# HGRN unit of a hybrid encoder block: inverse running products by scans, and a state chain with one VectorE operation per chunk

## The chip, the cores and the metric

The kernel runs on one core of a Trainium2 chip. A core has five engines that each work through a queue of their own in order: TensorE (PE, matmuls; PEld is its loading of weights), VectorE (DVE), ScalarE (ACT), GpSimd (POOL) and SyncE (SP, which here only issues transfers). They meet through semaphores. The metric is the device time of one execution in microseconds, and less is better.

## The reference

One layer of a bidirectional encoder over 1024 tokens of width 1024: a combined projection of 11776 columns, dilated attention, a gated linear recurrence (HGRN2) in both directions, a gated merge, a feed-forward part, and layer norms. The part that matters here is the recurrence. It has 8 heads with 128 keys and 128 values each, and is computed in chunks:

```python
cum = jnp.cumsum(logf.reshape(b, h, n, c, kd), axis=3)
q_dec = q * jnp.exp(cum)
k_inv = k * jnp.exp(-cum)
a = jnp.einsum('bhnik,bhnjk->bhnij', q_dec, k_inv)
a = jnp.where(causal_in_chunk, a, 0.0)
o_intra = jnp.einsum('bhnij,bhnjv->bhniv', a, v)
u = jnp.einsum('bhnck,bhncv->bhnkv', k * jnp.exp(cum_last - cum), v)
def step(state, inp):
    d, uu = inp
    return d[..., None] * state + uu, state
o_inter = jnp.einsum('bhnck,bhnkv->bhncv', q_dec, s_start)
```

So each gate f needs its running product within a chunk, the inverse of that product, and a state that is carried from chunk to chunk with one multiplication by the chunk's whole product.

## The kernel before

**Stages.** Phase 0 normalises the input (up to about 75 us of the profile). Phase 1 (up to about 1200 us) streams the combined projection: `stream` takes four column tiles at a time through a Strassen-Winograd scheme of seven block products, and every product is done as three matmuls (high x high, L244; high x low, L245; low x high, L246) over weights that are split into a rounded high part (`w_hi`, L205, ScalarE) and the rest (`w_lo`, L209, GpSimd). Four pairs of `w_hi`, `w_lo` are kept. Sums of weight blocks are made on VectorE and GpSimd (L477 to L482). Results leave the PSUM banks `pj0` to `pj3` through evacuations on VectorE (L392, L403, L417, L419) and ScalarE (L390, L500). Phases 2 and 3 are the merge and the feed-forward part.

**Side units.** Beside the projection, and on the same engines, phase 1 runs units of side work as soon as the columns that they need are there: eight HGRN units (one per head, `hgrn_side`) and eight attention units. A unit is a Python generator; each `yield n` lets `n` products of the stream be written before it goes on. The HGRN units fall, two by two, into the stretches from about 100, 400, 650 and 900 us.

**What sets the order.** The program is not written out by hand: a planner (`schedule_with_timeline_sim=True`) places each engine's instructions ahead of time by its own idea of their durations and by priority; evacuations of the projection and the preparation of weights are raised by `evac_ahead = 1000`. At run time each engine keeps the order that the planner gave it.

**An HGRN unit.** The tokens of a head lie in 8 groups of 128 along the free axis, `d` is the direction. A group is split into a near half and a far half of 64 tokens, and the running products start at the border between them, so that they stay within range. `hgrn_dir` makes the gates f on ScalarE (L930 to L936: `Identity` with scale `ga` and bias `gb` of a stored tanh) into `A` (the far half, 64 wide) and `B` (the near half, 66 wide), sets their first or last columns to zero on GpSimd (L928 to L934), and turns them into running products in place with a scan on VectorE (L942). The scan computes `state = f * state + d1`, where the table `d1` is zero but for a one at each group's start: so a zero in f and a one in `d1` restart the product. Then four reciprocals of 128x256 on VectorE (L953, L956) give the inverse products in `qd`; GpSimd multiplies the keys by `B` (L950) and by the inverse of `A` (L954), VectorE the queries by `A` (L957) and by the inverse of `B` (L958). `dec` takes the two halves' whole products of each group (L962, L963).

`hgrn_keys` transposes the keys through PSUM. `hgrn_states` makes the states that each group starts from: matmuls of keys and values into two PSUM banks (tag `sd`, of which there are four for all side work), then a chain on VectorE with two operations per group: add the decayed state before (L998) and decay the sum (L999; L996 for the first). ScalarE copies each state, scaled by `dec`, into `S` (L990). `hgrn_scores` and `hgrn_out` do the rest (L1012 to L1038). `S` of direction 0 takes the slot that held `A`, `S` of direction 1 that of `B` of direction 0.

Small buffers of 128x512 (`half`, five in rotation) are shared by the transposed keys, the scores, the output of the units and attention's bias tables.

Of the kernel before, what the change touches and what calls it, by code (L numbers as in the profile page):

```python
# [10 lines left out]
F32 = mybir.dt.float32  # L11
F32R = mybir.dt.float32r
I32 = mybir.dt.int32
AF = mybir.ActivationFunctionType
OP = mybir.AluOpType
# [19 lines left out]
CQ = 0.5 * 128 ** -0.5  # L35
# [44 lines left out]
class Block:  # L80
# [836 lines left out]

    def hgrn_dir(self, h, d, st):

        nc = self.nc  # L920
        ga, gb, gna = (z[:, d, h:h + 1] for z in (self.ga, self.gb, self.gna))
        t3 = st[f"t{d}"].rearrange("p (c i) -> p c i", i=128)
        q3 = st["q"].rearrange("p (c i) -> p c i", i=128)

        A = st["fa"][:, HALF * d:HALF * d + HALF].rearrange("p (c i) -> p c i", i=64)
        B = self.slot(7 + d, "fb", (8, 66))
        if d == 0:
            nc.gpsimd.memset(A[:, :, 0:1], 0.0)  # L928
            nc.gpsimd.memset(B[:, :, 65:66], 0.0)
            nc.scalar.activation(A[:, :, 1:64], t3[:, :, 65:128], AF.Identity, bias=gb, scale=ga)  # L930
            nc.scalar.activation(B[:, :, 0:65], t3[:, :, 0:65], AF.Identity, bias=gb, scale=ga)
        else:
            nc.gpsimd.memset(A[:, :, 63:64], 0.0)
            nc.gpsimd.memset(B[:, :, 0:1], 0.0)  # L934
            nc.scalar.activation(A[:, :, 0:63], t3[:, :, 0:63], AF.Identity, bias=gb, scale=ga)
            nc.scalar.activation(B[:, :, 1:66], t3[:, :, 63:128], AF.Identity, bias=gb, scale=ga)  # L936
        nc.gpsimd.tensor_scalar(t3, t3, gna, ga, op0=OP.mult, op1=OP.add)

        def scan(f, n, rev):
            f = f.rearrange("p c i -> p (c i)")  # L940
            f = f[:, ::-1] if rev else f
            nc.vector.tensor_tensor_scan(f, f, self.d1[n], 0.0, op0=OP.mult, op1=OP.add)  # L942

        scan(A, 64, d == 1)
        scan(B, 66, d == 0)
        far = slice(64, 128) if d == 0 else slice(0, 64)
        near = slice(0, 64) if d == 0 else slice(64, 128)
        R = B[:, :, 1:65]
        qd = self.slot(2 + 2 * d, "qd", (8, 128))
        nc.gpsimd.tensor_mul(t3[:, :, near], t3[:, :, near], R)  # L950
        yield
        for c in (slice(0, 4), slice(4, 8)):
            nc.vector.reciprocal(qd[:, c, far], A[:, c])  # L953
        nc.gpsimd.tensor_mul(t3[:, :, far], t3[:, :, far], qd[:, :, far])  # L954
        for c in (slice(0, 4), slice(4, 8)):
            nc.vector.reciprocal(qd[:, c, near], R[:, c])  # L956
        nc.vector.scalar_tensor_tensor(qd[:, :, far], q3[:, :, far], CQ, A, op0=OP.mult, op1=OP.mult)  # L957
        nc.vector.scalar_tensor_tensor(qd[:, :, near], q3[:, :, near], CQ, qd[:, :, near], op0=OP.mult, op1=OP.mult)  # L958
        st["qd", d], st["ki", d] = qd, t3

        dec = st["dec", d] = self.smt.tile([128, 2, 8], F32, name="dec", tag="dec", bufs=4)
        nc.gpsimd.tensor_copy(dec[:, 0, :], A[:, :, 63 if d == 0 else 0])  # L962
        nc.gpsimd.tensor_copy(dec[:, 1, :], B[:, :, 0 if d == 0 else 65])  # L963

    def hgrn_keys(self, st, d):

        nc, out = self.nc, []
        for b in (0, 1) if d == 0 else (1, 0):
            pt, kT = self.ps_sd(), self.half3("hkT")
            for k in range(4):  # L970
                nc.tensor.transpose(pt[:, 128 * k:128 * (k + 1)], st["ki", d][:, 4 * b + k, :], self.ident)
            nc.scalar.copy(kT, pt.rearrange("p (k c) -> p k c", k=4))
            out.append(kT)
        return out

    def hgrn_states(self, st, d, kT, vT):

        nc, dec = self.nc, st["dec", d]
        S = self.slot(6 + d, "hS", (8, 128))
        cs = list(range(8)) if d == 0 else list(range(7, -1, -1))  # L980
        E = None
        for b in range(2):
            ps = self.ps_sd().rearrange("p (k c) -> p k c", k=4)
            part = cs[4 * b:4 * b + 4]
            for jj, c in enumerate(part):
                if c != cs[-1]:
                    nc.tensor.matmul(ps[:, jj, :], kT[b][:, c % 4, :], vT[:, c, :], start=True, stop=True)  # L987
            for jj, c in enumerate(part):
                if E is not None:
                    nc.scalar.activation(S[:, c, :], E, AF.Copy, scale=dec[:, 1, c:c + 1])  # L990
                if c == cs[-1]:
                    continue

                En = self.sm.tile([128, 128], F32, name="hR", tag="hR", bufs=3)
                if E is None:
                    nc.vector.tensor_scalar(En, ps[:, jj, :], dec[:, 0, c:c + 1], None, op0=OP.mult)  # L996
                else:
                    nc.vector.scalar_tensor_tensor(En, E, dec[:, 1, c:c + 1], ps[:, jj, :], op0=OP.mult, op1=OP.add)  # L998
                    nc.vector.tensor_scalar(En, En, dec[:, 0, c:c + 1], None, op0=OP.mult)  # L999
                E = En  # L1000
        return S

    def hgrn_scores(self, st, b):
# [722 lines left out]
```

## Time and profile before

| | us |
|---|---|
| median of 3 runs (lowest, highest) | 2131.55 (2130.61, 2132.82) |
| span of the profiled execution | 2135.9 |
| TensorE busy (95% of the span) | 2032.5 |
| VectorE busy (65%) | 1386.7 |
| GpSimd busy (51%) | 1090.4 |
| ScalarE busy (43%) | 918.9 |

The profile is of one more execution; it gives its span from the first to the last instruction and no other time of it. A group's row reads: line, engine, operation, output<-inputs, shapes, count | busy us in all, mean ns of one | idle time of the engine just before them and what ended it. A row of the waits reads: engine and line that waited <- engine and line that ended the wait: us in all, times, longest. A row of a timeline reads: start, duration, engine, line, operation, and in brackets the idle time before it. Matmuls overlap, so their durations do not add up; the distance of their starts is what they cost.

### The profile page before, as it was taken

How to read it: one execution, taken by the hardware profiler on the slowest of the kernel's cores; microseconds unless marked ns; L12 is line 12 of the kernel's file. 1: busy time of each engine (PE TensorE's matmuls, PEld its weight loads, DVE VectorE, ACT ScalarE, POOL GpSimd, SP SyncE). 2: the span in 40 equal slices, each digit the busy share in tenths (PEclk: the TensorE clock that was granted, in tenths of full speed). 3: DMA queues.
4: the chain of work that ended last, by engine and by line, in shares of the span. 5: the costliest groups of instructions: out<-in, count | busy, mean ns of one | idle time of the engine just before them, and what ended most of it. 6: DMA issues, size and time to landing. Idle time of an engine off the chain costs nothing.

```text
span 2135.9 us, 30950 instructions
## 1 busy us (share of the span) xinstructions
PE 2032.5 (95%) x10941; PEld 1678.8 (79%) x10941; DVE 1386.7 (65%) x2228; ACT 918.9 (43%) x1864; POOL 1090.4 (51%) x882
## 2 busy tenths in 40 slices
PE   4799999999999999989999899999999999999998
PEld 3678787878878888868888688878788888888876
DVE  7666746776468754677536722336867677767777
ACT  6544445444554435443355332134433333334542
POOL 3465653565535764466644764353656666630012
PEclk9899999999999999999999999999999999999999
DMA  5343452434424453333433855244434334348433
GB/s 206 103 125 103 131 159 89 141 110 150 140 90 139 129 170 122 121 118 114 156 111 117 286 191 185 87 138 143 148 109 158 129 130 142 119 153 305 158 89 124
DMA packets 273885, 301.10 MB, mean 141 GB/s; under 512 B 14081, under 2 KB 205378, under 8 KB 273730
## 3 DMA queue, kind: packets, MB, share of 16 engines
q1 hardware_dynamic: 266272, 273.73, 39.9%
q10 hardware_dynamic: 7458, 25.40, 3.0%
q8 instruction: 86, 1.41, 0.3%
q14 instruction: 69, 0.57, 0.1%
HBM read 200.25 MB, written 98.83 MB: 140 GB/s over the span
## 4 chain that ended last, share of the span: by engine, by line
PE 62%; DVE 6%; issue 3%; DMA 3%; POOL 2%; ACT 1%; SPq 0%; ACTq 0%; DVEq 0%; POOLq 0%
PE pj L244 13%; PE pj L245 13%; PE pj L246 13%; PE sd L245 6%; PE sd L244 6%; PE sd L246 6%; POOL w_lo L209 1%; PE sd L1038 1%; PE sd L987 1%; DMA a<-ah 1%; DVE qd L956 1%; DVE qd L953 1%; POOL att_lo L209 0%; PE sd L643 0%; DVE hR L999 0%
## 5 line engine op out<-in xcount | busy, mean ns | idle before, releaser
L209 POOL TENSOR_TENSOR w_lo<-wa,w_hi 128x512 fp32r<-128x512 f32 x276 | 384.4, 1400 | 278.0 <-ACT w_hi L205 267.3
L205 ACT CAST w_hi<-wa 128x512 fp32r<-128x512 f32 x276 | 170.1, 618 | 231.1 <-PE pj L245 171.8
L209 POOL TENSOR_TENSOR w_lo<-wsum,w_hi 128x512 fp32r<-128x512 f32 x88 | 128.9, 1474 | 113.0 <-PE sd L246 60.7
L200 POOL TENSOR_TENSOR mv<-mv,mhalf 128x1 f32<-128x1 f32 x24 | 17.3, 723 | 228.9 <-DVE mv L199 225.7
L209 POOL TENSOR_TENSOR w_lo<-f_raw,w_hi 128x512 fp32r<-128x512 f32 x66 | 102.0, 1555 | 56.0 <-ACT w_hi L205 54.8
L244 PE MATMUL pj<-xt1hi,w_hi 128*128 128x512 f32 x260 | 105.0, 405 | 14.4 <-ACT xt1hi L205 6.9
L205 ACT CAST w_hi<-wsum 128x512 fp32r<-128x512 f32 x88 | 54.7, 621 | 124.6 <-PE sd L245 116.8
L245 PE MATMUL pj<-xt1lo,w_hi 128*128 128x512 f32 x260 | 103.5, 398 | 4.5 <-DVE xt1lo L209 4.5
L246 PE MATMUL pj<-xb22hi,w_lo 128*128 128x512 f32 x260 | 101.8, 391 | 1.6 <-POOL w_lo L209 1.6
L478 POOL TENSOR_TENSOR wa<-wa,wa 128x512 f32<-128x512 f32 x46 | 65.3, 1421 | 74.0 <-DVE ws L477 63.0
L246 PE MATMUL pj<-xt1hi,w_lo 128*128 128x512 f32 x260 | 102.9, 396 | 0.0
L244 PE MATMUL pj<-xb22hi,w_hi 128*128 128x512 f32 x260 | 102.5, 394 | 0.0
L245 PE MATMUL pj<-xb22lo,w_hi 128*128 128x512 f32 x260 | 101.8, 391 | 0.0
L209 POOL TENSOR_TENSOR w_lo<-ws,w_hi 128x512 fp32r<-128x512 f32 x46 | 67.3, 1467 | 64.2 <-ACT w_hi L205 63.9
L205 ACT CAST gwsum<-a_raw 128x512 fp32r<-128x512 f32 (+1 forms) x78 | 47.7, 616 | 100.9 <-PE pj L245 43.6
L500 ACT COPY wkeep<-pj 128x512 f32<-128x512 f32 x138 | 80.2, 581 | 11.4 <-DVE evh L392 5.9
L209 DVE TENSOR_TENSOR gwkeep<-a_raw,gwsum 128x512 fp32r<-128x512 f32 (+1 forms) x78 | 57.6, 739 | 41.1 <-ACT gwsum L205 38.2
L244 PE MATMUL pj<-xb11hi,w_hi 128*128 128x512 f32 x192 | 78.8, 412 | 4.9 <-DVE wkeep L417 3.4
L403 DVE TENSOR_TENSOR evh<-wkeep,pj 128x512 f32<-128x512 f32 x48 | 32.6, 680 | 76.4 <-PE pj L246 56.3
L244 PE MATMUL pj<-xt4hi,w_hi 128*128 128x512 f32 x192 | 77.1, 402 | 2.5 <-DVE evh L392 2.5
L246 PE MATMUL pj<-xt2hi,w_lo 128*128 128x512 f32 x192 | 75.7, 394 | 3.8 <-POOL w_lo L209 3.8
L990 ACT ACTIVATE hS<-hR,dec 128x128 f32<-128x128 f32 x112 | 44.5, 402 | 80.8 <-DVE hR L999 56.7
(406 smaller groups left out, 6608.3 us busy)
## 6 DMA issues: line engine op xcount, KB each, us to landing
wa<-in_w_in_dram SPq DMA_DIRECT2D x184, 256.0 KB, 3.1
f_raw<-in_w_ffn_in_dram SPq DMA_DIRECT2D x44, 512.0 KB, 4.2
a_raw<-gd SPq DMA_DIRECT2D x30, 512.0 KB, 3.8
gd<-fc SPq DMA_DIRECT2D x44, 256.0 KB, 2.0
gd<-fs SPq DMA_DIRECT2D x33, 256.0 KB, 2.1
tg<-evh SPq DMA_DIRECT2D x32, 256.0 KB, 2.9
tg<-tg SPq DMA_DIRECT2D x16, 512.0 KB, 3.8
y<-ahs SPq DMA_DIRECT2D x16, 512.0 KB, 5.3
```

The source lines that it names most:

```text
L205: nc.scalar.copy(hi, src)
L209: ins = e.tensor_sub(lo, src, hi.bitcast(F32))
L244: nc.tensor.matmul(ps, whi, xhi, start=first, stop=False, **kw)
L245: nc.tensor.matmul(ps, whi, xlo, start=False, stop=False, **kw)
L246: nc.tensor.matmul(ps, wlo, xhi, start=False, stop=last, **kw)
L403: nc.vector.tensor_add(t, add, ps)
L478: nc.gpsimd.tensor_sub(a["a21"], a["a11"], a["a21"])
L500: nc.scalar.copy(t, ps)
L953: nc.vector.reciprocal(qd[:, c, far], A[:, c])
L956: nc.vector.reciprocal(qd[:, c, near], R[:, c])
L987: nc.tensor.matmul(ps[:, jj, :], kT[b][:, c % 4, :], vT[:, c, :], start=True, stop=True)
L990: nc.scalar.activation(S[:, c, :], E, AF.Copy, scale=dec[:, 1, c:c + 1])
```

## The change

The diff touches `hgrn_dir` and `hgrn_states`.

In `hgrn_dir` the inverse products no longer come from reciprocals of the whole arrays. Two more buffers, `X` and `Y`, are filled with the same gates, shifted by one token, and scanned in the opposite direction, starting from the reciprocal of the group's whole product (128x8 values) in place of one. A product from the far end back to a token, divided by the whole product, is the inverse of the product up to that token. The starting values are written into the ones of the table `d1` (`first`), and a memset sets them to one again before the next direction. The queries of the near half now read `Y` instead of a part of `qd`.

In `hgrn_states` ScalarE takes each group's matmul result out of PSUM, already decayed by `dec[:, 0]`, into the slot of `S` that the next group will use. The chain on VectorE is then one operation per group, with `dec[:, 2]`, the product of the two decays, made by GpSimd. ScalarE scales the result by `dec[:, 1]` into `S`, and scales the first state in place.

```diff
+        X, Y = (self.half(n).rearrange("p (c i) -> p c i", i=64) for n in ("hx", "hy"))
+
+        def gate(out, src):
+            nc.scalar.activation(out, src, AF.Identity, bias=gb, scale=ga)
...
+            nc.gpsimd.memset(X[:, :, 63:64], 0.0)
+            nc.gpsimd.memset(Y[:, :, 0:1], 0.0)
+            gate(X[:, :, 0:63], t3[:, :, 65:128])
+            gate(Y[:, :, 1:64], t3[:, :, 1:64])
...
+        first = self.d1[64].rearrange("p (c i) -> p c i", i=64)[:, :, 0]
...
+        def inverse(f, total, rev):
+
+            nc.vector.reciprocal(first, total[:, ::-1] if rev else total)
+            scan(f, 64, rev)
+
+        nc.vector.memset(first, 1.0)
         scan(A, 64, d == 1)
         scan(B, 66, d == 0)
...
-        for c in (slice(0, 4), slice(4, 8)):
-            nc.vector.reciprocal(qd[:, c, far], A[:, c])
-        nc.gpsimd.tensor_mul(t3[:, :, far], t3[:, :, far], qd[:, :, far])
-        for c in (slice(0, 4), slice(4, 8)):
-            nc.vector.reciprocal(qd[:, c, near], R[:, c])
+        inverse(X, A[:, :, 63 if d == 0 else 0], d == 0)
+        nc.gpsimd.tensor_mul(t3[:, :, far], t3[:, :, far], X)
+        inverse(Y, R[:, :, 0 if d == 0 else 63], d == 1)
         nc.vector.scalar_tensor_tensor(qd[:, :, far], q3[:, :, far], CQ, A, op0=OP.mult, op1=OP.mult)
-        nc.vector.scalar_tensor_tensor(qd[:, :, near], q3[:, :, near], CQ, qd[:, :, near], op0=OP.mult, op1=OP.mult)
+        nc.vector.scalar_tensor_tensor(qd[:, :, near], q3[:, :, near], CQ, Y, op0=OP.mult, op1=OP.mult)
...
+        nc.gpsimd.tensor_mul(dec[:, 2, :], dec[:, 0, :], dec[:, 1, :])
...
-            for jj, c in enumerate(part):
-                if E is not None:
-                    nc.scalar.activation(S[:, c, :], E, AF.Copy, scale=dec[:, 1, c:c + 1])
-                if c == cs[-1]:
-                    continue
-
-                En = self.sm.tile([128, 128], F32, name="hR", tag="hR", bufs=3)
+            part = [(jj, c, cs[4 * b + jj + 1]) for jj, c in enumerate(cs[4 * b:4 * b + 4]) if c != cs[-1]]
+            for jj, c, _ in part:
+                nc.tensor.matmul(ps[:, jj, :], kT[b][:, c % 4, :], vT[:, c, :], start=True, stop=True)
+            for jj, c, after in part:
+                nc.scalar.activation(S[:, after, :], ps[:, jj, :], AF.Copy, scale=dec[:, 0, c:c + 1])
+            for jj, c, after in part:
                 if E is None:
-                    nc.vector.tensor_scalar(En, ps[:, jj, :], dec[:, 0, c:c + 1], None, op0=OP.mult)
+                    E = S[:, after, :]
                 else:
-                    nc.vector.scalar_tensor_tensor(En, E, dec[:, 1, c:c + 1], ps[:, jj, :], op0=OP.mult, op1=OP.add)
-                    nc.vector.tensor_scalar(En, En, dec[:, 0, c:c + 1], None, op0=OP.mult)
-                E = En
+                    En = self.sm.tile([128, 128], F32, name="hR", tag="hR", bufs=3)
+                    nc.vector.scalar_tensor_tensor(En, E, dec[:, 2, c:c + 1], S[:, after, :], op0=OP.mult, op1=OP.add)
+                    E = En
+                if after != cs[1]:
+                    nc.scalar.activation(S[:, after, :], E, AF.Copy, scale=dec[:, 1, after:after + 1])
+                    if after == cs[2]:
+                        nc.scalar.activation(S[:, cs[1], :], S[:, cs[1], :], AF.Copy, scale=dec[:, 1, cs[1]:cs[1] + 1])
```

More of the change, by code (lines that the diff above doesn't have):

```diff
@@ L926, in hgrn_dir @@
         B = self.slot(7 + d, "fb", (8, 66))
+        qd = self.slot(2 + 2 * d, "qd", (8, 128))
+        far = slice(64, 128) if d == 0 else slice(0, 64)
+        near = slice(0, 64) if d == 0 else slice(64, 128)
+        X, Y = (self.half(n).rearrange("p (c i) -> p c i", i=64) for n in ("hx", "hy"))
+        def gate(out, src):
+            nc.scalar.activation(out, src, AF.Identity, bias=gb, scale=ga)
         if d == 0:
@@ L929, in hgrn_dir @@
             nc.gpsimd.memset(B[:, :, 65:66], 0.0)
-            nc.scalar.activation(A[:, :, 1:64], t3[:, :, 65:128], AF.Identity, bias=gb, scale=ga)
-            nc.scalar.activation(B[:, :, 0:65], t3[:, :, 0:65], AF.Identity, bias=gb, scale=ga)
+            gate(A[:, :, 1:64], t3[:, :, 65:128])
+            gate(B[:, :, 0:65], t3[:, :, 0:65])
+            nc.gpsimd.memset(X[:, :, 63:64], 0.0)
+            nc.gpsimd.memset(Y[:, :, 0:1], 0.0)
+            gate(X[:, :, 0:63], t3[:, :, 65:128])
+            gate(Y[:, :, 1:64], t3[:, :, 1:64])
         else:
@@ L934, in hgrn_dir @@
             nc.gpsimd.memset(B[:, :, 0:1], 0.0)
-            nc.scalar.activation(A[:, :, 0:63], t3[:, :, 0:63], AF.Identity, bias=gb, scale=ga)
-            nc.scalar.activation(B[:, :, 1:66], t3[:, :, 63:128], AF.Identity, bias=gb, scale=ga)
+            gate(A[:, :, 0:63], t3[:, :, 0:63])
+            gate(B[:, :, 1:66], t3[:, :, 63:128])
+            nc.gpsimd.memset(X[:, :, 0:1], 0.0)
+            nc.gpsimd.memset(Y[:, :, 63:64], 0.0)
+            gate(X[:, :, 1:64], t3[:, :, 0:63])
+            gate(Y[:, :, 0:63], t3[:, :, 64:127])
         nc.gpsimd.tensor_scalar(t3, t3, gna, ga, op0=OP.mult, op1=OP.add)
+        first = self.d1[64].rearrange("p (c i) -> p c i", i=64)[:, :, 0]
         def scan(f, n, rev):
@@ L942, in scan @@
             nc.vector.tensor_tensor_scan(f, f, self.d1[n], 0.0, op0=OP.mult, op1=OP.add)
+        def inverse(f, total, rev):
+            nc.vector.reciprocal(first, total[:, ::-1] if rev else total)
+            scan(f, 64, rev)
+        nc.vector.memset(first, 1.0)
         scan(A, 64, d == 1)
         scan(B, 66, d == 0)
-        far = slice(64, 128) if d == 0 else slice(0, 64)
-        near = slice(0, 64) if d == 0 else slice(64, 128)
         R = B[:, :, 1:65]
-        qd = self.slot(2 + 2 * d, "qd", (8, 128))
         nc.gpsimd.tensor_mul(t3[:, :, near], t3[:, :, near], R)
         yield
-        for c in (slice(0, 4), slice(4, 8)):
-            nc.vector.reciprocal(qd[:, c, far], A[:, c])
-        nc.gpsimd.tensor_mul(t3[:, :, far], t3[:, :, far], qd[:, :, far])
-        for c in (slice(0, 4), slice(4, 8)):
-            nc.vector.reciprocal(qd[:, c, near], R[:, c])
+        inverse(X, A[:, :, 63 if d == 0 else 0], d == 0)
+        nc.gpsimd.tensor_mul(t3[:, :, far], t3[:, :, far], X)
+        inverse(Y, R[:, :, 0 if d == 0 else 63], d == 1)
         nc.vector.scalar_tensor_tensor(qd[:, :, far], q3[:, :, far], CQ, A, op0=OP.mult, op1=OP.mult)
-        nc.vector.scalar_tensor_tensor(qd[:, :, near], q3[:, :, near], CQ, qd[:, :, near], op0=OP.mult, op1=OP.mult)
+        nc.vector.scalar_tensor_tensor(qd[:, :, near], q3[:, :, near], CQ, Y, op0=OP.mult, op1=OP.mult)
         st["qd", d], st["ki", d] = qd, t3
-        dec = st["dec", d] = self.smt.tile([128, 2, 8], F32, name="dec", tag="dec", bufs=4)
+        dec = st["dec", d] = self.smt.tile([128, 3, 8], F32, name="dec", tag="dec", bufs=4)
         nc.gpsimd.tensor_copy(dec[:, 0, :], A[:, :, 63 if d == 0 else 0])
         nc.gpsimd.tensor_copy(dec[:, 1, :], B[:, :, 0 if d == 0 else 65])
+        nc.gpsimd.tensor_mul(dec[:, 2, :], dec[:, 0, :], dec[:, 1, :])
     def hgrn_keys(self, st, d):
@@ L983, in hgrn_states @@
             ps = self.ps_sd().rearrange("p (k c) -> p k c", k=4)
-            part = cs[4 * b:4 * b + 4]
-            for jj, c in enumerate(part):
-                if c != cs[-1]:
-                    nc.tensor.matmul(ps[:, jj, :], kT[b][:, c % 4, :], vT[:, c, :], start=True, stop=True)
-            for jj, c in enumerate(part):
-                if E is not None:
-                    nc.scalar.activation(S[:, c, :], E, AF.Copy, scale=dec[:, 1, c:c + 1])
-                if c == cs[-1]:
-                    continue
-                En = self.sm.tile([128, 128], F32, name="hR", tag="hR", bufs=3)
+            part = [(jj, c, cs[4 * b + jj + 1]) for jj, c in enumerate(cs[4 * b:4 * b + 4]) if c != cs[-1]]
[4 more added lines that the diff above has]
+            for jj, c, after in part:
                 if E is None:
-                    nc.vector.tensor_scalar(En, ps[:, jj, :], dec[:, 0, c:c + 1], None, op0=OP.mult)
+                    E = S[:, after, :]
                 else:
-                    nc.vector.scalar_tensor_tensor(En, E, dec[:, 1, c:c + 1], ps[:, jj, :], op0=OP.mult, op1=OP.add)
-                    nc.vector.tensor_scalar(En, En, dec[:, 0, c:c + 1], None, op0=OP.mult)
-                E = En
+                    En = self.sm.tile([128, 128], F32, name="hR", tag="hR", bufs=3)
[5 more added lines that the diff above has]
+                        nc.scalar.activation(S[:, cs[1], :], S[:, cs[1], :], AF.Copy, scale=dec[:, 1, cs[1]:cs[1] + 1])
         return S
```

## The prediction

> **What bounds the kernel.** I read the page's busy shares and its chain first, then the waits of TensorE inside the stage that holds the change (90 to 1170 us), then the timelines around the longest of those waits.
>
> ```profile
> PE 2032.5 (95%) x10941; PEld 1678.8 (79%) x10941; DVE 1386.7 (65%) x2228; ACT 918.9 (43%) x1864; POOL 1090.4 (51%) x882
> ...
> PE 62%; DVE 6%; issue 3%; DMA 3%; POOL 2%; ACT 1%; SPq 0%; ACTq 0%; DVEq 0%; POOLq 0%
> ```
>
> TensorE is busy 95% of the span and is nearly all of the chain. The change leaves every matmul as it is, so it can move the end only through the 5% in which TensorE stands still. What of that lies in the stage is in its waits:
>
> ```profile
> PE sd L852 <- DVE p L838: 8.1, 6, 2.4
> PE sd L1015 <- DVE hR L998: 7.1, 4, 4.0
> PE pj L244 <- DVE wkeep L417: 5.4, 3, 3.4
> PE pj L244 <- DVE evh L392: 4.7, 5, 2.1
> PE pj L244 <- DVE evh L403: 3.3, 1, 3.3
> ...
> PE pj L246 <- POOL w_lo L209: 2.2, 1, 2.2
> ```
>
> The first row is attention and is not touched. The next four, 20.5 us, end with VectorE in the HGRN units: L1015 is the score matmul that waits for a PSUM bank which the state chain (L998) still reads; the three at L244 are projection matmuls that wait for a bank whose evacuation stands in VectorE's queue. TensorE's timeline has the largest of both kinds, and what stands around one of them:
>
> ```profile
> 117.67 0.47 PE L244 MATMUL pj<-xt1hi,w_hi 128*128 128x512 f32 x1 [1.60 <-DVE wkeep L417]
> ...
> 125.72 0.47 PE L244 MATMUL pj<-xt1hi,w_hi 128*128 128x512 f32 x1 [3.31 <-DVE evh L403]
> ...
> 404.60 0.39 PE L246 MATMUL pj<-xt4hi,w_lo 128*128 128x512 f32 x1
> ...
> 405.28 0.39 PE L246 MATMUL pj<-xt4hi,w_lo 128*128 128x512 f32 x1
> ...
> 408.63 0.47 PE L244 MATMUL pj<-xt4hi,w_hi 128*128 128x512 f32 x1 [2.08 <-DVE evh L392]
> ...
> 410.01 0.63 PE L246 MATMUL pj<-xt4hi,w_lo 128*128 128x512 f32 x1
> ...
> 412.57 0.63 PE L246 MATMUL pj<-xt4hi,w_lo 128*128 128x512 f32 x1
> ...
> 468.29 0.77 PE L244 MATMUL pj<-xb11hi,w_hi 128*128 128x512 f32 x1 [3.38 <-DVE wkeep L417]
> ...
> 954.06 0.37 PE L1015 MATMUL sd<-qd,t 128*64 128x64 f32 x1 [4.04 <-DVE hR L998]
> ```
>
> and VectorE's timeline shows what the evacuation of 408.63 stood behind, the last PSUM read of the chain before 954.06, and a pair of reciprocals that the part on GpSimd needs:
>
> ```profile
> 107.23 3.30 DVE L956 RECIPROCAL qd<-fb 128x256 f32<-128x256 f32 x2
> ...
> 404.61 3.33 DVE L956 RECIPROCAL qd<-fb 128x256 f32<-128x256 f32 x2
> 407.86 0.62 DVE L392 TENSOR_TENSOR evh<-wkeep,pj 128x512 f32<-128x512 f32 x1
> ...
> 953.66 0.35 DVE L998 SCALAR_TENSOR_TENSOR hR<-hR,dec,sd 128x128 f32<-128x128 f32 x1
> ```
>
> From 410.01 to 412.57 seven matmuls start 0.427 us apart (2.56 / 6); from 404.60 to 405.28 four start 0.227 apart (0.68 / 3): TensorE runs at half rate for a while after a stall. I count 27 such matmuls behind HGRN stalls (8 after 125.72, 8 after 408.63, the others after 468.29 and 954.06 and one elsewhere), 27 x 0.20 = 5.4 us. So about 26 us hang on VectorE's lateness: 20.5 + 5.4.
>
> The Trainium skill (TensorE: Matmul & The Clock Gate, Part 1) has the clock drop to half after an idle window of about 3.4 us. By that only 954.06 would be followed by half rate, and the term below would be 1.0 us in place of 4.2. The trace disagrees: a stall of 2.08 us was enough.
>
> **The change, part by part.** The groups by line give the prices:
>
> ```profile
> L953 DVE RECIPROCAL qd<-fa 128x256 f32<-128x256 f32 x32 | 53.9, 1715 | 0.0
> L956 DVE RECIPROCAL qd<-fb 128x256 f32<-128x256 f32 x32 | 53.3, 1706 | 0.1
> L999 DVE TENSOR_SCALAR hR<-hR,dec 128x128 f32<-128x128 f32 x96 | 49.0, 511 | 2.8
> L998 DVE SCALAR_TENSOR_TENSOR hR<-hR,dec,sd 128x128 f32<-128x128 f32 x96 | 33.2, 346 | 7.8
> L990 ACT ACTIVATE hS<-hR,dec 128x128 f32<-128x128 f32 x112 | 44.5, 402 | 80.8 <-DVE hR L999 56.7 <-DVE hR L996 14.3 <-DVE qd L957 9.6
> L996 DVE TENSOR_SCALAR hR<-sd,dec 128x128 f32<-128x128 f32 x16 | 5.4, 338 | 7.8 <-PE sd L987 7.5
> L942 DVE TENSOR_TENSOR_SCAN fa<-fa,d 128x512 f32<-128x512 f32 x16 | 21.8, 1365 | 11.1 <-ACT fa L930 7.8 <-ACT fa L935 3.3
> ```
>
> ```profile
> L893 DVE RECIPROCAL lbm<-lbm 128x16 f32<-128x16 f32 x1 | 0.3, 253 | 0.0
> L928 POOL MEMSET fa<- x8: 106/112/116, 70.0 to 968.6; 128x8 f32 x8
> 100.78 0.81 ACT L931 ACTIVATE fb<-t,gb,ga 128x520 f32<-128x520 f32 x1
> 115.18 1.16 POOL L962 COPY dec<-fa 128x8 f32<-128x8 f32 x1
> ```
>
> VectorE, inverses: out go 64 reciprocals, 53.9 + 53.3 = 107.2 us. In come 32 scans of 512 at 1.365 = 43.7 us, 32 reciprocals of 128x8 at no more than the 0.253 of 128x16 = 8.1, and 16 memsets, at POOL's 0.11, 1.8. Net -53.6. VectorE, states: out go L999 and L996, 54.4 us; L998's 96 operations stay, but their third operand moves from PSUM to SBUF. No row shows that form: the ends are 0.346 (L998, as if the place did not matter) and 0.511 (L999, all in SBUF), and I take the middle, 0.43, since the new form shares its shape with one and its places with the other: +8 us. VectorE sheds 53.6 + 54.4 - 8 = about 100 us, 12.5 a unit.
>
> What of it lies on the path. *Scores:* a state bank is now let go after four (or three) ScalarE copies of 0.402 that follow the matmuls, and no longer at the end of a chain; the 7.1 us of L1015 go. Late next is S itself, which hgrn_out reads one step later; the chain per chunk falls from two operations to one, so I charge nothing; a chain as late as before would put the same 7.1 back. *Evacuations:* I compared VectorE's order in the two programs and added, at the prices above, the HGRN operations that stand between one projection evacuation (L392, L403, L417, L419) and the next. Stretches over 10 us fall from ten (longest 16.1) to five (longest 15.8). In the first unit the stretch ahead of the evacuation of 117.67 stays (13.8 before, 14.8 after), that of 125.72 falls from 8.1 to 2.8; the fourth and the last unit keep one (11.9, 13.2). So 3.31 and 2.08 go, and of the four smaller ones of L392 (4.7 less 2.08) and the third of L417 (5.4 less 1.60 and 3.38) all but the last unit's 1.4, 1.6 together; half of 3.38 goes; 1.60 stays: -8.7. *Half rate:* with the stalls at 125.72, 408.63 and 954.06 go 8 + 8 + 5 matmuls x 0.20 = -4.2. Together 7.1 + 8.7 + 4.2 = -20.0.
>
> ScalarE: 32 more gates at 0.81 = 26 us and 112 more scalings at 0.402 = 45 us. In the eight units' stretches (last fence) it is busy 197 of 454 us and comes to 268, 59%. I charge nothing. What hides it is that the rounding copies w_hi wait for a buffer from TensorE, not for ScalarE's queue. Without that cover the seven copies in a row (2.8 us) could stand ahead of w_hi 16 times: 45 us.
>
> GpSimd: 32 more memsets (3.6 us), 16 products of 128x8 (by the dec copies 0.19 to 1.16 each, 3 to 19 us). And it stands in the way of scans:
>
> ```profile
> 101.69 1.21 DVE L942 TENSOR_TENSOR_SCAN fa<-fa,d 128x512 f32<-128x512 f32 x1
> 111.84 2.31 DVE L942 TENSOR_TENSOR_SCAN fa<-fa,d 128x512 f32<-128x512 f32 x1
> ```
>
> ```profile
> 107.65 1.28 POOL L209 TENSOR_TENSOR w_lo<-wa,w_hi 128x512 fp32r<-128x512 f32 x1
> ...
> 113.03 2.20 POOL L209 TENSOR_TENSOR w_lo<-ws,w_hi 128x512 fp32r<-128x512 f32 x1
> ```
>
> w_lo took 1.28 us beside a reciprocal (107.23 to 110.45) and 2.20 beside the scan of 111.84, which itself took 2.31 where 1.21 is its free time. Four scans a unit more cost up to 4 x 0.92 = 3.7 us on GpSimd. The Trainium skill (SBUF — State Buffer, Who interferes with whom) states it as a rule: a VectorE instruction with two SBUF inputs contends with a GpSimd one that reads SBUF, one with a single SBUF input outside the two-port modes does not. The rows agree; it speaks against this change, which puts two-input scans where one-input reciprocals stood, and is the rule behind the second rival.
>
> ```profile
> L937 POOL TENSOR_SCALAR t<-t,gna,ga 128x1024 f32<-128x1024 f32 x16 | 33.3, 2082 | 5.0 <-ACT fb L936 2.2 <-ACT fa L930 1.7 <-ACT fb L931 1.1
> L950 POOL TENSOR_TENSOR t<-t,fb 128x512 f32<-128x512 f32 x16 | 21.7, 1358 | 0.2 <-DVE fb L942 0.2
> L954 POOL TENSOR_TENSOR t<-t,qd 128x512 f32<-128x512 f32 x16 | 20.6, 1289 | 0.9 <-DVE qd L953 0.8
> sum 454.00, PE 426.91 PEld 357.29 DVE 370.17 ACT 197.09 POOL 295.80; mean PE 53.36 PEld 44.66 DVE 46.27 ACT 24.64 POOL 36.98
> ```
>
> GpSimd is busy 296 of 454 us there, so the 4.5 to 6.5 us a unit mostly fit into its 20 us of gaps. But in the changed order the three key steps follow each other directly in every second unit (2.08 + 1.36 + 1.29 = 4.7 us, the last waiting for the new scan) with the next w_lo behind them, where w_lo stood between before. TensorE eats one weight block in 12 x 0.227 = 2.7 us. One stall of this kind is in the trace (2.2, above). I take 1.2 us a unit, +9.6, about half that stall in each; the ends are 0 and the second rival's 37.
>
> SP's transfers are the same in kind; only places in its order move. No price.
>
> **Sum.** -20.0 + 9.6 = -10.4 us. The profiled execution's span, 2135.9, becomes 2125.5. The three timed runs' median, 2131.55, lies 4.4 under that span; less 10.4 it gives 2121.
>
> **Rivals.** (1) The whole gain: no new stall, and all 25.9 us go, 2106. For it: ScalarE and GpSimd have room. Against: the long stretches that stay in four units. (2) GpSimd becomes late, slower: w_lo behind the three key steps comes 4.7 us later plus 3.7 of scan contention, less two weight blocks of lead, 5.4: a stall of 3.0 with 1.6 of half rate behind it (as after 408.63), 4.6 a unit, 37 in all; with the 20 gained it ends at +17, 2148. It decides from 2.5 us a unit on. For it: the rows of 113.03 and 111.84, and GpSimd's queue being strictly in order. Against: 20 us of gaps a unit. (3) No change: the planner fixed both orders ahead of time, and evacuations stay as late as they were because HGRN work was moved up before them, as in the first unit: 2131.
>
> **Numbers.** My forecast 0.45, (1) 0.12, (3) 0.15, (2) 0.28. Faster or slower by over 0.2% (4.3 us, about what this kernel's runs can tell): forecast and (1) make faster 0.57, (3) same 0.15, (2) slower 0.28. The range 2106 to 2145 leaves out the far half of (1) and the upper third of (2); the forecast's own range is 2113 to 2127.
>
> **What would show it.** Right: the waits of the score matmul for hR gone; L392, L403 and L417 under 6 us together; VectorE near 1287 us busy; w_lo's waits under 12 us. Wrong: a new row of TensorE waiting for w_lo of 20 us or more, or scans and w_lo near 2.2 us on average; hgrn_out waiting for hS.

## The result, and the profile after

The changed kernel is slower. Its median is 2141.92 us against 2132.44 us of the kernel before (7 runs each), a ratio of 1.0041 with a 95% interval of 1.0029 to 1.0052, or +8.7 us by the ratio (the medians are 9.5 apart). The profiled execution's span is 2142.4 us (2135.9 before), 6.5 more.

The page of the changed kernel shows these busy times and, below them, the shares of the chain that ended last:

```profile
PE 2032.0 (95%) x10941; PEld 1673.1 (78%) x10941; DVE 1316.5 (61%) x2132; ACT 964.6 (45%) x2008; POOL 1123.3 (52%) x930
...
PE 72%; POOL 8%; DVE 7%; issue 6%; DMA 5%; ACT 1%; SPq 0%; ACTq 0%; POOLq 0%; DVEq 0%
```

TensorE has the same work as before, as it must. VectorE sheds 70 us and GpSimd gains 33, and GpSimd's share of the chain goes from 2% to 8%. TensorE's idle time is the span less 2032: 103.4 us before, 110.4 now. That is the whole loss between the two profiled executions. Its waits in the stage from 90 to 1170 us say who it now waits for:

```profile
PE pj L246 <- POOL w_lo L209: 22.2, 16, 2.8
PE sd L852 <- DVE p L838: 7.8, 6, 2.6
PE sd L1008 <- ACT hkT L993: 5.5, 5, 2.1
PE sd L992 <- POOL t L975: 2.6, 2, 1.6
PE pj L244 <- DVE wkeep L417: 1.2, 1, 1.2
...
PE pj L244 <- DVE evh L392: 0.3, 1, 0.3
```

The waits on VectorE that made up 20.5 us are down to 1.5 (the score matmul's row is gone altogether). In their place stand 22.2 us of waits for `w_lo`, GpSimd's part of the weight split, which were 2.2 before. GpSimd's groups in the stage, the three key steps, the small `dec` operations, and one group of VectorE's scans:

```profile
L954 POOL TENSOR_SCALAR t<-t,gna,ga 128x1024 f32<-128x1024 f32 x16 | 29.8, 1863 | 1.5 <-ACT fb L934 0.8 <-DMA wa<-in_w_in_dram 0.7
L975 POOL TENSOR_TENSOR t<-t,hx 128x512 f32<-128x512 f32 x16 | 27.9, 1747 | 0.0
L972 POOL TENSOR_TENSOR t<-t,fb 128x512 f32<-128x512 f32 x16 | 26.3, 1647 | 0.3
...
L983 POOL COPY dec<-fb 128x8 f32<-128x8 f32 x16 | 11.6, 722 | 10.6 <-DVE fb L961 10.4
...
L984 POOL TENSOR_TENSOR dec<-dec 128x8 f32<-128x8 f32 x16 | 7.3, 454 | 0.4
```

```profile
L961 DVE TENSOR_TENSOR_SCAN hy<-hy,d 128x512 f32<-128x512 f32 x16 | 28.0, 1750 | 0.9
```

The keys' product with the inverse took 1.29 us a piece before (L954 there) and 1.75 now (L975), the one with `B` 1.36 and now 1.65; the key gate alone got faster, from 2.08 to 1.86. The scans of `Y` got slower too: 1.75 us where an undisturbed one is 1.21. VectorE's timeline and GpSimd's show both sides in one place:

```profile
402.76 1.61 DVE L961 TENSOR_TENSOR_SCAN fa<-fa,d 128x512 f32<-128x512 f32 x1
...
404.98 1.63 DVE L977 SCALAR_TENSOR_TENSOR qd<-q,fa 128x512 f32<-128x512 f32 x1
406.54 2.20 DVE L961 TENSOR_TENSOR_SCAN hx<-hx,d 128x512 f32<-128x512 f32 x1
```

```profile
403.23 1.12 POOL L983 COPY dec<-fb 128x8 f32<-128x8 f32 x1
404.32 1.75 POOL L209 TENSOR_TENSOR w_lo<-wa,w_hi 128x512 fp32r<-128x512 f32 x1
...
407.63 2.20 POOL L209 TENSOR_TENSOR w_lo<-wa,w_hi 128x512 fp32r<-128x512 f32 x1
```

A copy of 8 values per partition takes 1.12 us there (0.19 in quiet places), and ends where the scan of 402.76 ends; the `w_lo` behind it then takes 1.75 in place of 1.28. TensorE stood still for 2.77 us until this `w_lo` was there (its matmul starts at 406.12). That scan is one of `A`, which the kernel before has too, with a copy of 1.15 us beside one (398.79). The added scan of 406.54 took 2.20 us in place of 1.21, and the `w_lo` that began during it 2.20 in place of 1.28.

The stage's account: VectorE's waits -19.0 us, `w_lo` +20.0, `hkT` (ScalarE's copies of the transposed keys) +2.9, the wait for the transposes' keys (L975, before L950) +1.7, sum +5.6. By windows, TensorE's idle time in the stage went from 35.8 to 41.9 us.

### The profile page after: what moved, and what is told of

Its sections match the earlier page's. It is cut to its first block, busy times and chain, and to the rows that moved or that the text cites. A ratio compares the mean times of both kernels' runs of the same rounds, so it can differ in the third digit from the quotient of the medians.

```text
span 2142.4 us, 31051 instructions
## 1 busy us (share of the span) xinstructions
PE 2032.0 (95%) x10941; PEld 1673.1 (78%) x10941; DVE 1316.5 (61%) x2132; ACT 964.6 (45%) x2008; POOL 1123.3 (52%) x930
## 4 chain that ended last, share of the span: by engine, by line
PE 72%; POOL 8%; DVE 7%; issue 6%; DMA 5%; ACT 1%; SPq 0%; ACTq 0%; POOLq 0%; DVEq 0%
PE pj L246 15%; PE pj L245 15%; PE pj L244 15%; PE sd L245 6%; PE sd L244 6%; PE sd L246 6%; POOL w_lo L209 4%; PE sd L1059 2%; DMA wa<-in_w_in_dram 1%; PE sd L1008 1%; POOL t L954 1%; POOL t L975 1%; DVE p L838 1%; DMA a<-ah 1%; DMA xt<-in_x_dram 1%
## 5 line engine op out<-in xcount | busy, mean ns | idle before, releaser
L209 POOL TENSOR_TENSOR w_lo<-wa,w_hi 128x512 fp32r<-128x512 f32 x276 | 392.6, 1431 | 243.9 <-ACT w_hi L205 230.2
L245 PE MATMUL pj<-xt1lo,w_hi 128*128 128x512 f32 x260 | 103.4, 398 | 4.5 <-DVE xt1lo L209 4.5
L477 DVE TENSOR_TENSOR ws<-wa,wa 128x512 f32<-128x512 f32 x46 | 40.6, 884 | 70.8 <-DMA wa<-in_w_in_dram 61.5
L246 PE MATMUL pj<-xb11hi,w_lo 128*128 128x512 f32 x192 | 77.7, 405 | 3.6 <-POOL w_lo L209 3.6
L392 DVE TENSOR_TENSOR evh<-wkeep,pj 128x512 f32<-128x512 f32 x66 | 58.2, 889 | 36.1 <-PE pj L246 25.8
```

The lines of the kernel that those rows point to most:

```text
L209: ins = e.tensor_sub(lo, src, hi.bitcast(F32))
L245: nc.tensor.matmul(ps, whi, xlo, start=False, stop=False, **kw)
L246: nc.tensor.matmul(ps, wlo, xhi, start=False, stop=last, **kw)
L392: nc.vector.tensor_tensor(o, self.order_src(add, g, kind), s, OP.add)
L477: nc.vector.tensor_add(a["s1"], a["a21"], a["a22"])
```

## The experiments

Theory A, formed on this profile, is that the 32 added scans hold up GpSimd where the reciprocals did not, so that `w_lo` comes late. Theory B is that it is GpSimd's added work and the order of its queue, whatever VectorE runs beside it. Theory C is that the new state chain costs, through ScalarE. Each run has its own runs of the kernel before to compare with, and differences in us are between the two medians. The median before is 2134.97 us for the first three runs and the key gate on ScalarE alone, 2134.70 for the two with the `dec` operations moved, 2133.62 for the other four.

**Only the scans.** `hgrn_dir` of the changed kernel, `hgrn_states` of the one before:

```diff
 def hgrn_states(self, st, d, kT, vT):
-        dec = st["dec", d] = self.smt.tile([128, 3, 8], F32, name="dec", tag="dec", bufs=4)
+        dec = st["dec", d] = self.smt.tile([128, 2, 8], F32, name="dec", tag="dec", bufs=4)
-        nc.gpsimd.tensor_mul(dec[:, 2, :], dec[:, 0, :], dec[:, 1, :])
```

> Only the scans in place of reciprocals; the state chain is the old one. Theory A (the scans hold the SBUF port that GpSimd needs, so w_lo comes late): TensorE's waits for w_lo in the stage stay near the 22 us of the whole change, the score matmul's waits for hR come back (about 7 us), time 2141 to 2150. Theory B (GpSimd's added work and the order of its queue, not the port): the same, 2141 to 2150. Theory C (the new state chain, with its 112 more ScalarE operations, is what costs): time within 4 us of before, 2128 to 2136, w_lo waits under 8 us.

2152.9 us, ratio 1.0082 (1.0070 to 1.0095): +17.9 us, slower than the whole change and just above the range that A and B gave. Two rows of TensorE's waits in its stage:

```profile
PE pj L246 <- POOL w_lo L209: 20.9, 16, 2.8
PE sd L1035 <- DVE hR L1018: 8.3, 4, 2.7
```

The new waits for `w_lo` come with the scans (and their gates and memsets), without the new chain. C falls as the main cause; A and B are not told apart by this run.

**Only the state chain.** The reverse: reciprocals as before, `hgrn_states` of the changed kernel with its third `dec`.

> Only the new state chain; reciprocals as before. Theories A and B: the score matmul's waits for hR (7 us before) go and nothing comes in their place, w_lo waits under 6 us, time 2123 to 2128. Theory C: time 2138 to 2145, with TensorE waiting for ScalarE or for w_lo behind ScalarE.

2128.2 us, ratio 0.9959 (0.9945 to 0.9974): a gain of 6.8 us, by the medians at the upper edge of what A and B gave. The score matmul's wait for the chain is gone from its list. What remains in the HGRN units is mostly VectorE's:

```profile
PE pj L244 <- DVE evh L392: 6.7, 4, 3.3
PE pj L244 <- DVE wkeep L417: 5.1, 2, 3.1
PE pj L246 <- POOL w_lo L209: 2.1, 1, 2.1
```

The two parts add up: 1.0082 and 0.9959 give 1.0041, which is the whole change.

**One input in place of two.** The whole change, but what follows the small reciprocal in `inverse` is a reciprocal of part of the buffer:

```diff
             nc.vector.reciprocal(first, total[:, ::-1] if rev else total)
-            scan(f, 64, rev)
+            nc.vector.reciprocal(f[:, :, 20:44], f[:, :, 20:44])
```

> The whole change, but each of the 32 added scans is replaced by a reciprocal in place of 128x192 values of the same buffer (left out: the inverse products themselves), about as long as a scan (192/256 x 1.71 = 1.29 us) but with one SBUF input. GpSimd's list of work is that of the whole change. Theory A: key steps on GpSimd fall from 1.65 and 1.75 us to near 1.3, TensorE's waits for w_lo fall from 22 to under 10 us, time 2120 to 2130. Theory B: w_lo waits stay at 16 us or more, time 2137 to 2143.

2115.19 us, ratio 0.9903 (0.9887 to 0.9918). This is a gain of 19.8 us. The waits for `w_lo` and the groups, of that run's stage:

```profile
PE pj L246 <- POOL w_lo L209: 5.9, 7, 2.4
```

```profile
L975 POOL TENSOR_TENSOR t<-t,hx 128x512 f32<-128x512 f32 x16 | 24.3, 1518 | 0.0
...
L984 POOL TENSOR_TENSOR dec<-dec 128x8 f32<-128x8 f32 x16 | 3.6, 231 | 0.4
```

```profile
L966 DVE RECIPROCAL hx<-hx 128x192 f32<-128x192 f32 x16 | 21.2, 1326 | 0.0
```

GpSimd has the same work to do, with gates, memsets and `dec` products, and is busy 619.7 us in the stage in place of 642.6; its `dec` product takes 0.23 us in place of 0.45. The key steps fall less far than A said (1.52 for L975, not 1.3); the other scans stay beside them, but whether that is the reason was not tried. The planner's order is not the same one: GpSimd's three key steps follow each other directly ahead of `w_lo` in two of the four second units and two of the first ones (in the whole change, in all four second ones). That leaves a doubt, and so does VectorE's time: 42 us of these reciprocals against 52 of scans.

**The same, longer.** Theory D is that doubt as a theory: the run was fast because VectorE had less to do. As above with `f[:, :, 14:50]`, 128x288 values.

> As the run with one-input reciprocals, but 128x288 of them in place of 128x192 (left out: the inverse products): each some 1.9 us, longer than the scans took (1.48 and 1.75). Theory A: VectorE's time is not what counts, w_lo waits stay under 10 us, time 2115 to 2128. Theory D (the shorter run won because VectorE was done sooner, 42 us against 52): w_lo waits and time go back to those of the whole change, 2135 or more.

2115.32 us, ratio 0.9910 (0.9896 to 0.9925).

```profile
PE pj L246 <- POOL w_lo L209: 6.7, 7, 2.3
```

```profile
L966 DVE RECIPROCAL hx<-hx 128x288 f32<-128x288 f32 x16 | 30.8, 1927 | 0.0
```

Each now takes longer than a scan of the whole change (1.93 and 1.90 us, 61 us in all), and the time and the waits stay where they were. VectorE's time is not what counts, and D falls.

**Two inputs without the change.** The kernel before, its reciprocals replaced by additions with both inputs in SBUF (`one` is the scan's table):

```diff
-            nc.vector.reciprocal(qd[:, c, far], A[:, c])
+            nc.vector.tensor_add(qd[:, :, far], A, one)
...
-            nc.vector.reciprocal(qd[:, c, near], R[:, c])
+            nc.vector.tensor_add(qd[:, :, near], R, one)
```

> The kernel before, nothing of the change in it, but each of its 64 reciprocals replaced by an addition of 128x512 with both inputs in SBUF (left out: the inverse products): some 0.68 us each undisturbed, 44 us in all, as the 32 scans. No added gates, memsets or products. Theory A: though VectorE sheds 60 us, GpSimd is held up: w_lo waits of 10 us or more (2.2 before), time 2128 to 2142. Theory B (GpSimd's added small work and the order of its queue): VectorE's relief shows unhindered, w_lo waits under 6 us, time 2112 to 2124.

2141.06 us, ratio 1.0028 (1.0015 to 1.0040). VectorE sheds 32 us in the stage (700.8 to 668.3), not 60, as the additions took 1.00 and 1.23 us a piece, not 0.68; and the kernel gets slower.

```profile
PE pj L246 <- POOL w_lo L209: 12.0, 9, 2.8
```

```profile
L937 POOL TENSOR_SCALAR t<-t,gna,ga 128x1024 f32<-128x1024 f32 x16 | 40.2, 2512 | 5.6 <-ACT fb L936 2.7 <-ACT fa L930 1.7 <-ACT fb L931 1.1
...
L963 POOL COPY dec<-fa 128x8 f32<-128x8 f32 x16 | 10.8, 677 | 9.1 <-DMA hg6g<-evh 4.9 <-DVE fa L942 4.1
```

GpSimd's work is that of the kernel before, nothing added, and it is 33 us busier in the stage (645.8 against 612.5): the key gate goes from 2.08 to 2.51 us, the copy from 0.31 to 0.68. This is theory A by itself, without the gates, memsets and products that B would need.

**The same inside each trace.** The planner's order differs between these runs, so a comparison inside one trace is the stronger one. `w_lo` always has the same shape. These are the ones of the stage that began while VectorE ran the named operation with 0.3 us or more of it to go, or that had nothing beside them on VectorE:

| beside `w_lo` on VectorE | run | number | us, mean (range) |
|---|---|---|---|
| nothing | changed kernel | 72 | 1.29 (1.25 to 1.30) |
| added scan, two inputs | changed kernel | 10 | 2.19 (2.16 to 2.21) |
| reciprocal 128x256, one input | kernel before | 34 | 1.29 (1.26 to 1.31) |
| reciprocal 128x192 and 128x288, one input | the two one-input runs | 9 and 18 | 1.29 (1.26 to 1.31) |
| addition, two inputs | two inputs without the change | 20 | 1.71 (1.57 to 1.77) |

The ranges of one-input and two-input operations do not meet. A `w_lo` lost 0.90 us to an added scan and nothing to a reciprocal.

**Relief for GpSimd.** Three runs take work off GpSimd in the changed kernel. The first moves the key gate to ScalarE:

```diff
-        nc.gpsimd.tensor_scalar(t3, t3, gna, ga, op0=OP.mult, op1=OP.add)
+        nc.scalar.activation(t3, t3, AF.Identity, bias=ga, scale=gna)
```

> The whole change, and the 16 key gates of 128x1024 (L954, 29.8 us on GpSimd) made by ScalarE. Theories A and B both have GpSimd as what is late: w_lo waits fall from 22 to under 10 us, time 2120 to 2132. Theory C: ScalarE, 22 us busier, makes it slower than the whole change, above 2142.

2128.79 us, ratio 0.9965 (0.9952 to 0.9978). The waits for `w_lo` fall from 22.2 to 13.1 us, not under 10, and TensorE's waits for `hkT`, ScalarE's copy, do not grow (2.3 us, 5.5 in the whole change). The second also takes the product with `X`:

```diff
-        nc.gpsimd.tensor_mul(t3[:, :, far], t3[:, :, far], X)
+        nc.vector.tensor_mul(t3[:, :, far], t3[:, :, far], X)
```

> The whole change, key gate on ScalarE, and the keys' product with X on VectorE in place of GpSimd (29 us off GpSimd, 11 to 20 on VectorE). Theory A, GpSimd's queue being what is late: waits for w_lo fall from 13 to under 8 us, time 2116 to 2126. If the VectorE product, which has two SBUF inputs itself, holds GpSimd up as much as it spares it: 2126 to 2132.

2122.08 us, ratio 0.9942 (0.9928 to 0.9956), faster than the kernel before and the changed one.

```profile
PE pj L246 <- POOL w_lo L209: 5.7, 4, 3.3
```

The third moves the small `dec` operations as well, the copies to ScalarE and the product to VectorE:

```diff
-        nc.gpsimd.tensor_copy(dec[:, 0, :], A[:, :, 63 if d == 0 else 0])
+        nc.scalar.copy(dec[:, 0, :], A[:, :, 63 if d == 0 else 0])
...
-        nc.gpsimd.tensor_mul(dec[:, 2, :], dec[:, 0, :], dec[:, 1, :])
+        nc.vector.tensor_mul(dec[:, 2, :], dec[:, 0, :], dec[:, 1, :])
```

> As the run with the key gate on ScalarE and the keys' product on VectorE (2122 us, ratio 0.9942), and the 48 small dec operations (28 us on GpSimd there, most of it waiting for the port) on ScalarE (copies) and VectorE (product). Theory A: GpSimd has only memsets and one key product left from the HGRN gates; waits for w_lo stay under 6 us, time 2114 to 2123. If the small operations were free on GpSimd: 2120 to 2126.

2128.61 us, ratio 0.9970 (0.9958 to 0.9983). Both readings missed: `w_lo` was in time and yet it is slower than the run before it.

```profile
PE sd L992 <- DVE t L975: 9.8, 3, 4.0
...
PE pj L246 <- POOL w_lo L209: 3.6, 4, 1.5
```

```profile
L984 DVE TENSOR_TENSOR dec<-dec 128x8 f32<-128x8 f32 x16 | 13.9, 866 | 0.0
```

TensorE now waits for VectorE's key product. The `dec` product on VectorE takes 0.87 us a piece where the small reciprocals of the same 128x8 took 0.20: 12 of the 16 end within 0.05 us of the end of the GpSimd operation that ran when they began, and the three with nothing beside them took 0.12 to 0.16 us. The waiting has moved to VectorE's side; that this is all of the loss to the run before was not isolated.

**Only the small operations moved.** The whole change with only the `dec` operations off GpSimd:

> The whole change with nothing but the 48 small dec operations moved off GpSimd (26.6 us busy there). They are 128x8 each, so what they cost is standing behind a scan. Theory A: they are part of what makes GpSimd late; waits for w_lo fall from 22 to 10 to 17 us, time 2132 to 2140. If they only fill gaps: w_lo waits 19 us or more, time 2139 to 2145.

2138.73 us, ratio 1.0023 (1.0013 to 1.0034), `w_lo` waits 17.4 us. By the waits they are a small part of the lateness, smaller than A had it (10 to 17 us); the time lies in A's range, but its interval overlaps that of the whole change.

**State chain and gate.** Reciprocals as before, the new state chain, and the key gate on ScalarE:

> The new state chain with the old reciprocals, and the key gate of 128x1024 on ScalarE. Theory A: nothing that GpSimd waits for is added and 31 us of its work are gone, so the waits for w_lo stay at 2 us or fall; what is left are evacuations behind reciprocals (13 us in the states-only run). Time 2120 to 2129, ratio to before 0.993 to 0.998. Against it, if ScalarE's 22 us more are what counts: above 2130.

2124.68 us, ratio 0.9953 (0.9939 to 0.9966). Its interval overlaps that of the states alone: without the scans, GpSimd is not what is late, and sparing it brings little. What is left are evacuation waits on VectorE, the largest row being

```profile
PE pj L244 <- DVE evh L392: 8.0, 3, 4.0
```

## Why the prediction was wrong

The forecast was -10.4 us, the measured difference is +8.7. The sum had two terms, -20.0 for TensorE's waits and +9.6 for GpSimd. The first came out at -19.0; the second was the step that failed.

**Scores, right.** -7.1 forecast. The row is gone in the changed kernel and in the states-only run, which is 6.8 us faster, and back at 8.3 in the scans-only run.

**Evacuations, right in kind and better than forecast.** -8.7 forecast; L392, L403 and L417 fell from 13.4 to 1.5 us, -11.9. The wait that was to stay at 1.60 us is there at 1.21 (118.26); the stretches of VectorE's order that I counted as staying late in the fourth and the last unit did not hurt. So the third rival, evacuations as late as before, is out.

**Half rate, wrong.** -4.2 forecast, nothing came. The old half-rate stretches went with their stalls, and new ones came behind the new stalls: 5 half-rate matmuls after 406.12, 8 after 487.14, 8 after 694.91, 5 after 1001.63, or 26 against the 27 that I had counted. The term belonged to stalls of any cause, and I gave it to VectorE's alone.

**VectorE's own time.** 100 us forecast, 70 measured. The scans took 1.48 and 1.75 us, not 1.365 (51.7 us, not 43.7), and the chain's operations 45.0 us for 96, not 41. About 15 us more is operations that the change left as they were and that took longer, 9 of it the sums of weight blocks (L477, L479, L482). Little hangs on it: the runs with one-input reciprocals of 42 and 61 us are equally fast.

**GpSimd, the step that failed.** I took 1.2 us a unit, +9.6, on the ground that 4.5 to 6.5 us a unit of added GpSimd time mostly fit into its 20 us of gaps. The added time was below that: 30.1 us in the stage, 3.8 a unit, and the price of a scan to a `w_lo` was right (0.92 forecast, 0.90 measured). But it did not fit. The gaps are an average over a unit's whole stretch, and the scans stand in the part of it in which GpSimd has no gaps: from 395.93 to 417 us its timeline has none at all. That could be seen beforehand: in the kernel before GpSimd has none from 397.40 to 416.77 either. With waits for `w_lo` (+20.0) and L975 (+1.7) the term measures 21.7 us, 2.7 a unit, above the 2.5 from which I had said the second rival decides. The rows for it stood in the prediction, `w_lo` at 1.28 and at 2.20 us; I priced the added time at its average and not where it falls.

**The second rival** is what happened, with the reason half right. It named the scan contention and the three key steps in a row ahead of `w_lo` in every second unit. The contention is shown, by the table inside the traces, and by the waits: with one-input operations in the scans' place `w_lo`'s waits fall to 5.9 and 6.7 us, and with two-input operations in the kernel before they rise to 12.0. The row of three is not what cost: the four rows begin at 207.66, 463.10, 727.38 and 979.56, and the first wait for `w_lo` behind each ends 22 us later or more. The second units have 7.2 of the 22.2 us (at 487.14, 753.05, 1001.63 and 1015.61). Its price was 37, measured 21.7.

**The first rival**, the whole gain of 25.9, did not come. The one-input runs, which leave the inverse products out, come nearest to it with 19.8 and 18.3; they still have 5.9 and 6.7 us of waits for `w_lo`.

**ScalarE, charged nothing, wrong by 2.9 us.** It gained 43 us in the stage, not 71, and the run that gave it 24 more was faster, so its busy time is not what counts. But TensorE's waits for `hkT` rose from 2.6 to 5.5 us, and the trace shows why: of the five waits, those at 241.96, 694.91 and 1019.91, 4.3 us together, are for a copy whose transposes were done 9 to 11 us before it started. It stood in ScalarE's queue behind the scalings of the new chain (L1019, L1021), which waited 7.0 to 9.6 us for the chain's first operation on VectorE (L1016). The row is 2.1 us with the scans alone and 1.0 with the chain alone, so it takes both halves of the change.

**The rule of the Trainium skill** (SBUF — State Buffer, Who interferes with whom), that a VectorE instruction with two SBUF inputs contends with a GpSimd one that reads SBUF and one with a single input outside the two-port modes does not, agrees with the traces here: `w_lo` took 2.19 and 1.71 us beside two-input operations and 1.29 beside one-input ones. **The clock rule** of the Trainium skill (TensorE: Matmul & The Clock Gate, Part 1), an idle window of about 3.4 us, does not decide by the length of the stall here: 2.77 us before 406.12 and 2.11 before 694.91 were followed by half rate, 2.20 before 925.06 was not. What decides can be worked out from the granted clock in the traces, which goes to half for 3.41 us or a multiple of it, at times that lie on a grid of 3.41 us (in the changed kernel from 405.57, 487.49, 695.70 and 1002.90). In the cell of the grid before these TensorE stood idle 2.2, 2.4, 2.1 and 2.1 us; the stall before 925.06 lies across a border, 1.5 us in one cell and 0.7 in the next. Over the stage of all twelve traces every cell at full clock with over 1.9 us idle was followed by half rate, and none with under 1.6; in between both came.

## What to carry to other kernels

Count for a VectorE operation not only its time but how many of its inputs lie in SBUF, when GpSimd has a deadline: here 52 us of two-input scans, with their gates, in place of 107 us of one-input reciprocals cost 17.9 us, though VectorE was the busier engine of the two. Price an engine's slack at the place where the new work stands, not as an average over the stage. And take a change apart: the state chain alone gains 0.41%, the scans alone lose 0.82%, and the whole change with the key gate on ScalarE and one key product on VectorE is 0.58% faster than the kernel before (interval 0.44% to 0.72%).

## What the runs showed of the hardware that was not expected

An operation on 8 values per partition is not small beside the other engine's long ones: the `dec` copy of `B` averaged 0.36 us before and 0.72 in the changed kernel, and the `dec` product averaged 0.45 us on GpSimd in the changed kernel, 0.23 on GpSimd beside the one-input reciprocals, and 0.87 on VectorE, where most of it was standing behind GpSimd. Moving it from one engine to the other moved the waiting with it.

TensorE's drop to half rate followed a cell of the 3.41 us grid with about half of it idle or more, so a stall of 2.1 us could cost 8 half-rate matmuls and one of 2.2 us none.
